# A two-layer hybrid-head decoder on one core: NSA's SBUF pool opened below mLSTM's instead of above it

## The chip, the core and the metric

The kernel runs on one core of one Trainium2 chip. The core has engines that work side by side and each take their instructions in a fixed order: TensorE (PE: matmuls and transposes; PEld is its weight load), VectorE (DVE), ScalarE (ACT), GpSimd (POOL) and SyncE (SP, which here only issues transfers). They meet at semaphores; SBUF is the working memory, PSUM holds matmul results. The metric is the device time of one execution in microseconds (us). All times below come from the runs of the kernel before and from one profiled execution of it.

## The reference, cut to what is computed

Two layers over 512 tokens of width 1024, float32. Each layer projects the normed input to four mixers of four heads of width 64 each, adds their joint output projection to the residual, then adds a cross attention over 256 memory rows and a SwiGLU of width 2816.

```python
for layer in range(2):
    cols = rms_norm(x, g) @ w_in               # split into the four mixers' columns
    m0 = hgrn2_mixer(...)   # gated linear recurrence in chunks of 64, then norm and gate
    m1 = dsa_mixer(...)     # an index picks the top keys of each query, attention over them
    m2 = nsa_mixer(...)     # compressed, selected and windowed attention, gated
    m3 = mlstm_mixer(...)   # matrix-memory recurrence in chunks of 64, then norm and gate
    x = x + concat(m0, m1, m2, m3) @ w_out
    x = x + cross_attention(rms_norm(x), mem)
    x = x + swiglu(rms_norm(x))
```

## The kernel before, in words

**Products.** The residual lives in SBUF transposed, as eight tiles `xT` of 128x512. Each float32 product is made of three matmuls on halves: `xh`,`xl` are the high and low part of an operand, `wh`,`wl` those of a weight (lines L339 to L341 where tokens come out on rows, L329 to L331 where features do; the latter take 128x512). `wh` is written by ACT (L292), `wl` by POOL (L293) from a raw tile `wr` (L277); some weights are split once and come back from memory later (`whl`, L303).

**Stages of a layer.** Stage A interleaves the DSA index and its selection (DVE, L696 and L697), NSA, mLSTM and all input projections. Stage B follows: `load_x` fetches the residual again into `xT` (L405, eight transfers of 256 KB on SP's queue, which takes them in order with all weight transfers), and then three generators are interleaved by cost: `dsa_attn` (DSA's attention: scores L552, exponentials, products L574, transposed back by L605), `hg` (HGRN2: gates L837 to L841 on DVE, products L856 inside chunks, L902 to L930 across them, output norm and gate `h_g` on DVE), and a chain of `out_stage(0)`, `xa_kv`, `out_stage(1)`. `out_stage(s)` is the part of the output projection that belongs to a mixer pair: stage 0 takes NSA's and mLSTM's results (`mo`: NSA's halves are made by ACT and by DVE in L1277, mLSTM's and HGRN2's are first transposed by PE in L1281), stage 1 takes DSA's, stage 2 HGRN2's and runs with the cross attention that follows. In layer 0 `hg` first loads a mask of levels, `lvf` (L826, two transfers), and casts it on DVE (L827); `h_tf`, which the gates read, takes over the mask's staging slots. DSA's keys are made ready by L716 (sum of squares of its latent `d_ckv`, squared by ACT in L713) and L723 (its product with `wukv`), then by a norm and a rotation on DVE.

**Space.** Pools are stacked on the left side of SBUF; a pool that is opened next lies above the one before, and `left.close()` frees both of stage A's. In the space of NSA and mLSTM stage B then puts, from the bottom, `xT`, the pool of `hg` and the pool `dat` of DSA's attention. `reuse_waits="tile"` makes the first writer of a new tile wait for the last users of just those old tiles that lay where it lies. A tile scheduler orders the instructions of each engine ahead of time, from the priorities that the mixes give and from these waits.

Of the kernel before, what the change touches and what calls it, by code (L numbers as in the profile page):

```python
# [206 lines left out]
class Kernel:  # L207
# [1329 lines left out]
    def run(self):  # L1537
        nc = self.nc
        late = ExitStack()
        for l in range(DEPTH):  # L1540
            self.l = l
            banks = ExitStack()
            self.banks(banks, "ba", tp=1, sc=2, o=1, dt=1, mb=1)
            if l == 0:
                self.load_x(self.i["xT"])
            self.layer_consts()
            if l == 0:
                self.open_sq()
            right, index = ExitStack(), ExitStack()
            self.hqf = self.pool(right, "hgqf", side="right")  # L1550
            self.mo = {2: self.t(self.mp, "mo2", [128, 2, S], bufs=1), 3: self.t(self.mp, "mo3", [128, TB, 256], bufs=1)}
            pd = self.pool(index, "dsa", n2=4, n4=0, side="right")
            self.alias[id(pd)] = {"tp": "dt", "sc": "dt"}
            acc = self.dsa_in(pd)
            if l == 0:
                self.setup()
            self.rstd(row=True)
            if l == 0:
                xd = self.i["xT"]
            else:  # L1560
                xd = self.tc.dram_tile([D, S], FT, name=f"xd{l}")
                for c in range(KC):
                    nc.sync.dma_start(xd[c * 128:c * 128 + 128, :], self.xT[c])
            self.xpool.close()
            late.close()
            late, left = ExitStack(), ExitStack()
            pk = self.pool(late, "keep")
            pm = self.pool(left, "ml", n2=3)
            pn = self.pool(left, "nsa", n2=3, n4=1)
            self.alias[id(pn)] = {}  # L1570
            self.hin = None
            for tb in range(TB):
                with self.first():
                    nc.scalar.activation(self.d_idx[:, tb], acc[tb], AF.Copy, scale=self.rcol[:, tb:tb + 1])
            self.weave((self.chain(self.dsa(pd, pk), self.hg_space(index, right)), COST["dsa"]),
                       (self.chain(self.nsa_in(pn),
                                   self.mix((self.nsa(pn), COST["nsa"]),
                                            (self.chain(self.ml_in(pm),
                                                        self.mix((self.ml(pm), COST["ml"]),
                                                                 (self.chain(self.ml_in2(pm), self.dsa_in2(pk), self.hg_in()), COST["in"]))),  # L1580
                                             COST["mlin"]))),
                        COST["two"]))
            left.close()
            banks.close()
            banks = ExitStack()
            self.banks(banks, "bb", tp=1, sc=1, o=1, dt=1, hb=2)
            self.load_x(xd)
            ph = self.pool(left, "hg", n2=2, n4=0)
            pa = self.pool(left, "dat", n2=3, n4=0)
            px = self.pool(right, "xk", n2=2, n4=1, side="right")  # L1590
            self.alias[id(pa)] = {"tp": "dt"}
            self.attn_done = False
            self.weave((self.dsa_attn(pa), COST["attn"]), (self.hg(ph), COST["hg"]),
                       (self.chain(self.out_stage(0), self.xa_kv(px), self.out_stage(1)), COST["out"]))
            left.close()
            banks.close()
            banks = ExitStack()
            self.banks(banks, "bc", tp=2, sc=2, o=2)
            self.open_sq()
            with ExitStack() as e:  # L1600
                p = self.pool(e, "xa")
                rest = self.xa_in(p)
                right.close()
                self.raws = (self.pool(right, "raw", side="right"), RAWS)
                self.all(self.xa(p, self.pool(e, "xo", side="right"), rest))
            with ExitStack() as e:
                self.ffn(self.pool(e, "ffn"))
            self.raws = (self.wp, 3)
            right.close()
            banks.close()  # L1610
        self.xpool.close()
        late.close()
# [18 lines left out]
```

## Time and profile before

| what | value |
|---|---|
| median of 3 runs | 1689.66 us (1684.8 to 1689.67) |
| the profiled execution | 1688.9 us, of which the span is 1687.1 us |
| mean granted clock of TensorE | 0.972 |
| PE busy | 1607.5 us, 95% of the span |
| DVE, POOL, ACT busy | 924.0, 799.1, 712.5 us (55%, 47%, 42%) |
| chain of work that ended last | PE 84%, DVE 8%, issue 3%, DMA, POOL and ACT 2% each |

PE is busy almost throughout, and its matmuls are the chain that ends last for most of the span. What is left to win or to lose by order alone lies in the some 80 us in which PE stands still, and in the stretches where its clock is granted at half.

### The profile page before, as it was taken

What the parts mean: (1) busy time and instruction counts of PE and PEld (TensorE: products, weight loads), DVE (VectorE), ACT (ScalarE), POOL (GpSimd) and SP (SyncE); (2) the same over time, 40 slices, a digit from 0 to 9 for tenths busy, and PEclk for the clock granted to TensorE, in tenths of its full rate; (3) what the DMA queues carried; (4) which work ended last, traced back from release to release, by engine and by line L of the source; (5) the groups of instructions that cost most, each with busy time, mean ns of one, the idle gap of its engine ahead of it and who ended that gap; (6) DMA issues with size and microseconds to landing.
All of it is one profiled execution on the core that took longest, in us unless ns stands there. A gap on an engine that the chain in (4) does not pass through costs nothing.

```text
span 1687.1 us, 25484 instructions
## 1 busy us (share of the span) xinstructions
PE 1607.5 (95%) x9256; PEld 1333.1 (79%) x9262; DVE 924.0 (55%) x1760; ACT 712.5 (42%) x1525; POOL 799.1 (47%) x698
## 2 busy tenths in 40 slices
PE   7899998998899989999999999989998999999999
PEld 7778877777788868888898887677877888888887
DVE  5697688876755330344225884879786644123420
ACT  5555453454654443443324433423665433223321
POOL 5664333456448888874412010144672344444442
PEclk9999997999999999999999999979999999999999
DMA  5342212212338999953355734122131233333331
GB/s 160 89 119 76 70 34 84 57 38 85 112 121 286 305 316 319 333 192 93 105 156 178 262 107 132 58 95 57 45 119 38 66 97 90 92 100 94 94 103 66
DMA packets 114365, 212.72 MB, mean 126 GB/s; under 512 B 12984, under 2 KB 30136, under 8 KB 114240
## 3 DMA queue, kind: packets, MB, share of 16 engines
q1 hardware_dynamic: 111888, 206.11, 38.7%
q10 hardware_dynamic: 2032, 3.94, 0.7%
q8 instruction: 73, 1.20, 0.3%
q0 software_dynamic: 320, 1.05, 0.2%
q14 instruction: 52, 0.43, 0.1%
HBM read 170.69 MB, written 40.35 MB: 125 GB/s over the span
## 4 chain that ended last, share of the span: by engine, by line
PE 84%; DVE 8%; issue 3%; DMA 2%; POOL 2%; ACT 2%; SPq 0%; POOLq 0%; ACTq 0%; DVEq 0%
PE acc L329 14%; PE acc L331 14%; PE acc L330 14%; PE sc L330 5%; PE sc L331 5%; PE sc L329 5%; PE acc L339 3%; PE acc L340 3%; PE acc L341 3%; PE hb L856 3%; PE o L574 2%; PE sc L552 2%; PE tp L493 2%; PE mb L1048 1%; PE dt L493 1%
## 5 line engine op out<-in xcount | busy, mean ns | idle before, releaser
L293 POOL TENSOR_TENSOR wl<-wr,wh 128x512 fp32r<-128x512 f32 (+5 forms) x432 | 551.7, 1285 | 459.3 <-ACT wh L292 447.8
L292 ACT ACTIVATE wh<-wr 128x512 fp32r<-128x512 f32 (+5 forms) x432 | 252.1, 592 | 336.2 <-PE acc L330 149.2
L329 PE MATMUL acc<-xh,wh 128*128 128x512 f32 (+1 forms) x704 | 276.9, 395 | 0.8 <-ACT xh L1283 0.5
L330 PE MATMUL acc<-xl,wh 128*128 128x512 f32 (+1 forms) x704 | 274.6, 390 | 2.9 <-DVE xl L1277 2.9
L331 PE MATMUL acc<-xh,wl 128*128 128x512 f32 (+1 forms) x704 | 275.4, 392 | 0.4 <-POOL wl L293 0.4
L466 DVE TENSOR_TENSOR xT<-acc,xT 128x512 f32<-128x512 f32 (+1 forms) x112 | 68.1, 611 | 214.4 <-PE acc L331 213.6
L329 PEld LDWEIGHTS acc<-xh,wh 128*128 128x128 f32 x704 | 133.9, 191 | 32.1 <-issue 1.7
L330 PEld LDWEIGHTS acc<-xl,wh 128*128 128x128 f32 x704 | 134.3, 191 | 30.8 <-DVE xl L1277 4.0
L331 PEld LDWEIGHTS acc<-xh,wl 128*128 128x128 f32 x704 | 134.1, 190 | 28.7 <-POOL wl L293 1.1
L329 PE MATMUL acc<-f_gh,wh 128*128 128x512 f32 x352 | 139.1, 397 | 6.8 <-ACT f_gh L1491 6.8
L339 PE MATMUL acc<-wh,xh 128*128 128x256 f32 (+2 forms) x480 | 140.6, 296 | 4.9 <-DMA wh<-whl 3.8
L331 PE MATMUL acc<-f_gh,wl 128*128 128x512 f32 x352 | 139.7, 398 | 0.7 <-POOL wl L293 0.7
L330 PE MATMUL sc<-xl,wh 128*128 128x512 f32 x352 | 139.7, 397 | 0.0
L330 PE MATMUL acc<-f_gl,wh 128*128 128x512 f32 x352 | 139.5, 398 | 0.0
L340 PE MATMUL acc<-wl,xh 128*128 128x256 f32 (+2 forms) x480 | 139.0, 291 | 0.0
L331 PE MATMUL sc<-xh,wl 128*128 128x512 f32 x352 | 139.0, 395 | 0.0
L329 PE MATMUL sc<-xh,wh 128*128 128x512 f32 x352 | 138.0, 393 | 0.0
L341 PE MATMUL acc<-wh,xl 128*128 128x256 f32 (+2 forms) x480 | 137.4, 288 | 0.0
L318 POOL TENSOR_TENSOR phl<-pr,phl 128x512 fp32r<-128x512 f32 (+3 forms) x72 | 95.1, 1321 | 35.0 <-ACT phl L317 31.8
L317 ACT ACTIVATE phl<-pr 128x512 fp32r<-128x512 f32 (+3 forms) x72 | 44.2, 613 | 133.9 <-DMA pr<-in_wst 117.2
L339 PEld LDWEIGHTS acc<-wh,xh 128*128 128x128 f32 x480 | 92.9, 194 | 8.8 <-DMA wh<-whl 4.3
L340 PEld LDWEIGHTS acc<-wl,xh 128*128 128x128 f32 x480 | 93.3, 195 | 1.4 <-issue 0.8
(407 smaller groups left out, 3159.8 us busy)
## 6 DMA issues: line engine op xcount, KB each, us to landing
wr<-in_wst SPq DMA_DIRECT2D x332, 256.0 KB, 2.7
whl<-phl SPq DMA_DIRECT2D x52, 512.0 KB, 3.9
pr<-in_wst SPq DMA_DIRECT2D x52, 256.0 KB, 4.1
wh<-whl SPq DMA_DIRECT2D x52, 256.0 KB, 4.1
wl<-whl SPq DMA_DIRECT2D x52, 256.0 KB, 4.4
wr<-in_wst SPq DMA_DIRECT2D x48, 128.0 KB, 2.2
wr<-in_wst SPq DMA_DIRECT2D x32, 192.0 KB, 2.4
whl<-phl SPq DMA_DIRECT2D x8, 524.0 KB, 3.7
```

The lines of the kernel that those rows point to most:

```text
L292: nc.scalar.activation(hi, raw, AF.Copy)
L293: nc.gpsimd.tensor_tensor(lo, raw, hi.bitcast(FT), op=OP.subtract)
L318: nc.gpsimd.tensor_tensor(both[:, 1], raw, both[:, 0].bitcast(FT), op=OP.subtract)
L329: self.nc.tensor.matmul(acc, wh, xh, start=(j == 0), stop=False)
L330: self.nc.tensor.matmul(acc, wh, xl, start=False, stop=False)
L331: self.nc.tensor.matmul(acc, wl, xh, start=False, stop=(j == n - 1))
L339: self.nc.tensor.matmul(acc, xh[:, s], wh, start=(first and j == 0), stop=False)
L340: self.nc.tensor.matmul(acc, xh[:, s], wl, start=False, stop=False)
L341: self.nc.tensor.matmul(acc, xl[:, s], wh, start=False, stop=(last and j == n - 1))
L466: self.nc.vector.tensor_add(self.xT[c][:, cols], acc, self.xT[c][:, cols])
L493: self.nc.tensor.transpose(p[:rows, j * 128:j * 128 + 128], src(j), self.ident)
L856: nc.tensor.matmul(sc[s0:s1, b + t0:b + t1], kk[po:po + 64, b + s0:b + s1], qq[po:po + 64, b + t0:b + t1], start=True, stop=True)
```

## The change

The two lines that open the pools of stage A in each layer are exchanged, so that NSA's pool lies at the bottom and mLSTM's above it.

```diff
             pk = self.pool(late, "keep")
+            pn = self.pool(left, "nsa", n2=3, n4=1)
             pm = self.pool(left, "ml", n2=3)
-            pn = self.pool(left, "nsa", n2=3, n4=1)
             self.alias[id(pn)] = {}
```

In bytes of a partition, before: mLSTM at 108096 to 144970, NSA from 145024 to 195600. After: NSA at 108096 to 158650, mLSTM at 158656 to 195520. Stage B's tiles keep their places: `xT` at 108096 to 124480, the pool of `hg` at 130624 to 164480, that of DSA's attention at 164544 to 195200. Before, `xT` and most of `hg` lay on mLSTM's tiles and DSA's attention on NSA's; now `xT` and `hg` but for its upper end lie on NSA's, and DSA's attention on mLSTM's. No instruction is added to the computation or taken from it. The waits for old tiles differ, and with them the order on each engine. Three places follow.

**SP and DVE at the start of stage B, layer 0.** SP's rows with what they wait for (in brackets, the queue or engine whose semaphore it is): the first reload of the residual, and the two transfers of the mask. Before:

```order
L405 DMA xT_3248<-in_xT 128x512 [waits DMASW2_49,DVE_49]
...
L405 DMA xT_3255<-in_xT 128x512 [waits DMAHW1_49]
L826 DMA lvf<-in_levels 128x384 [waits DMAHW2_49,PE_49]
L826 DMA lvf<-in_levels 128x256 [waits DMAHW3_49]
L277 DMA wr<-in_wst 128x512 [waits DMAHW4_49,Pool_49]
```

After:

```order
L405 DMA xT_3248<-in_xT 128x512 [waits DMASW2_49,PE_49]
...
L405 DMA xT_3255<-in_xT 128x512 [waits DMAHW6_49]
L1307 DMA memT<-in_memT 128x256 [waits DMAHW7_49,DVE_49]
...
L720 DMA wukv<-in_wukv 128x128 [waits DMAHW1_49]
L826 DMA lvf<-in_levels 128x384 [waits DMAHW2_49]
L826 DMA lvf<-in_levels 128x256 [waits DMAHW3_49,DVE_49]
```

The first reload waited for DVE's last use of an mLSTM tile (`mo<-mo,m_tok`); it now waits for PE's last NSA product (L1161). The memory rows and `wukv` moved behind the reload. On DVE, at the same place, before:

```order
L351 TENSOR_TENSOR kv<-rope_3302,rope_3303 128x4x16
L503 CAST ks<-kv 128x4x64
L351 TENSOR_TENSOR ks<-kv,ks 128x4x64
L374 TENSOR_REDUCE q_st<-sq 128x4
L347 TENSOR_SCALAR rs_ms<-q_st 128x4
L827 CAST lv<-lvf 128x384
L827 CAST lv<-lvf 128x256
L837 TENSOR_SCALAR h_f<-h_tf,lbw 128x512
```

After:

```order
L351 TENSOR_TENSOR mo_106<-mo_106,m_tok 128x4x64
L718 TENSOR_SCALAR d_ckv<-d_ckv,cols 128x512
L827 CAST lv<-lvf 128x384
L827 CAST lv<-lvf 128x256
L837 TENSOR_SCALAR h_f<-h_tf,lbw 128x512
...
L874 TENSOR_TENSOR h_ks_3342<-h_k_3336,h_Fk_3338 128x512
L347 TENSOR_SCALAR rs_ms<-dt 128x4
L351 TENSOR_TENSOR kv<-dt,d_st_3273 128x512
```

The mask and the whole gate block of HGRN2 moved ahead of DSA's keys (`kv`). On PE, likewise, L716 and L723 moved from ahead of HGRN2's value and gate projections into them, and the first scores of DSA (L552) ten matmuls further into `out_stage(0)`.

**PE at the end of stage B, layer 0.** The rows from HGRN2's last products on (L928, L930), with its transposes L1281. Before, with seven L574 and four L605, DSA's last, some 85 rows higher:

```order
L928 MATMUL hb<-h_S_4159,h_q 128x128
L930 MATMUL hb<-h_v,h_aT_3384 128x64
L930 MATMUL hb<-h_v,h_aT_3515 128x64
L1281 MATMUL tp<-kc,h_g 128x128 x8
L329 MATMUL acc<-xh,wh 128x512 x2
L330 MATMUL acc<-xl,wh 128x512
```

After:

```order
L574 MATMUL o<-PT,kv 64x128 x7
L605 MATMUL dt<-kc,stat 64x128 x4
L928 MATMUL hb<-h_S_4133,h_q 128x128
...
L930 MATMUL hb<-h_v,h_aT_3515 128x64
L329 MATMUL acc<-xh,wh 128x512 x2
L1281 MATMUL tp<-kc,h_g 128x128 x4
...
L331 MATMUL acc<-xh,wl 128x512
L1281 MATMUL tp<-kc,h_g 128x128 x2
```

Before, the 48 matmuls of `out_stage(1)` were done between HGRN2's products, and its eight transposes stood together. Now DSA ends later, the 48 stand behind HGRN2's last product, and the transposes lie among them. Layer 1 has the same order at this place, with some transposes `tp<-kc,x_ks` beside.

**SP at the start of stage B, layer 1.** Before, four transfers of split weights (L303) stood in the middle of the reload:

```order
L405 DMA xT_11819<-xd_9031 128x512
L303 DMA wl<-whl_8428 128x512
L303 DMA wh<-whl_8428 128x512
L303 DMA wl<-whl_8546 128x512
L303 DMA wh<-whl_8546 128x512
L405 DMA xT_11820<-xd_9031 128x512
```

After:

```order
L405 DMA xT_11823<-xd_9031 128x512
L1307 DMA memT<-in_memT 128x256 x2
L720 DMA wukv<-in_wukv 128x128
L303 DMA wl<-whl_8428 128x512
L303 DMA wh<-whl_8428 128x512
L303 DMA wh<-whl_8546 128x512
L303 DMA wl<-whl_8546 128x512
```

They stand behind the whole reload now, which again waits for PE's L1161 instead of DVE's `mo<-mo,m_tok`.

**Elsewhere.** At the program's start ACT has one square `xsq` and two exponentials of `lbw` (L804) ahead of the first `wh`, which before stood behind it.

## Rows read from the trace of the kernel before

**Rows 1.** The page: busy time by engine; the chain that ended last.
```profile
PE 1607.5 (95%) x9256; PEld 1333.1 (79%) x9262; DVE 924.0 (55%) x1760; ACT 712.5 (42%) x1525; POOL 799.1 (47%) x698
...
PE 84%; DVE 8%; issue 3%; DMA 2%; POOL 2%; ACT 2%; SPq 0%; POOLq 0%; ACTq 0%; DVEq 0%
```
**Rows 2.** PE's waits over the whole span: us in total, times, longest.
```profile
PE acc L330 <- DVE xl L1277: 2.9, 2, 2.6
...
PE dt L723 <- DVE rs_ms L347: 1.0, 1, 1.0
...
PE hb L856 <- DVE h_q L841: 0.8, 1, 0.8
```
**Rows 3.** SP in order of time, layer 0: start, duration, transfers issued.
```profile
276.32 3.65 SPq L405 DMA_DIRECT2D xT<-in_xT  x8
280.07 0.85 SPq L826 DMA_DIRECT2D lvf<-in_levels  x2
```
**Rows 4.** DVE in order of time, layer 0, start of stage B: start, duration.
```profile
275.87 0.42 DVE L351 TENSOR_TENSOR mo<-mo,m_tok 128x256 f32<-128x256 f32 x1
...
285.31 2.35 DVE L827 CAST lv<-lvf 128x384 uint8<-128x384 f32 x2 [1.53 <-DMA lvf<-in_levels]
...
289.06 0.68 DVE L841 SCALAR_TENSOR_TENSOR h_q<-h_tq,h_q 128x512 f32<-128x512 f32 x1
```
**Rows 5.** PE in order of time, layer 0, start of stage B.
```profile
258.77 2.08 PE L1161 MATMUL dt<-n_eT,n_vbd 128*128 128x512 f32 x2 [0.69 <-DVE mo L351]
...
303.13 0.80 PE L330 MATMUL acc<-xl,wh 128*128 128x512 f32 x1 [2.57 <-DVE xl L1277]
...
308.31 0.40 PE L330 MATMUL acc<-xl,wh 128*128 128x512 f32 x1
```
**Rows 6.** PE in order of time, layer 0, end of stage B.
```profile
388.83 0.70 PE L605 MATMUL dt<-kc,stat 128*64 128x128 f32 x7
...
392.90 0.39 PE L331 MATMUL acc<-xh,wl 128*128 128x512 f32 x1
...
394.98 0.39 PE L331 MATMUL acc<-xh,wl 128*128 128x512 f32 x1
...
411.94 0.44 PE L1281 MATMUL tp<-kc,h_g 128*128 128x128 f32 x2 [1.75 <-DVE h_g L351]
414.54 0.69 PE L1281 MATMUL tp<-kc,h_g 128*128 128x128 f32 x2 [2.17 <-DVE h_g L351]
415.71 1.22 PE L329 MATMUL acc<-xh,wh 128*128 128x512 f32 x2 [0.47 <-ACT xh L1283]
416.73 0.63 PE L330 MATMUL acc<-xl,wh 128*128 128x512 f32 x1
...
420.57 0.58 PE L331 MATMUL acc<-xh,wl 128*128 128x512 f32 x1
```
**Rows 7.** ACT in order of time: DSA's last rows at that end.
```profile
390.96 0.51 ACT L616 ACTIVATE xh<-spread 128x128 fp32r<-128x128 f32 x2 [1.00 <-DVE spread L351]
```
**Rows 8.** SP in order of time, layer 1, start of stage B.
```profile
1114.09 2.87 SPq L405 DMA_DIRECT2D xT<-xd  x4
...
1118.47 0.38 SPq L303 DMA_DIRECT2D wh<-whl  x1
```
**Rows 9.** PE in order of time, layer 1, same place.
```profile
1122.87 0.58 PE L339 MATMUL acc<-wh,xh 128*128 128x256 f32 x1 [3.79 <-DMA wh<-whl]
...
1127.51 0.29 PE L339 MATMUL acc<-wh,xh 128*128 128x256 f32 x1
```
**Rows 10.** ACT in order of time, the start.
```profile
9.05 0.62 ACT L427 ACTIVATE xsq<-xT 128x512 f32<-128x512 f32 x1
...
10.18 0.29 ACT L804 ACTIVATE lbw<-lbw 128x4 f32<-128x4 f32 x2
```
**Rows 11.** DVE and POOL in order of time, layer 1, HGRN2's gates.
```profile
1118.64 1.75 DVE L841 SCALAR_TENSOR_TENSOR h_q<-h_tq,h_q 128x512 f32<-128x512 f32 x1
...
1118.13 1.72 POOL L293 TENSOR_TENSOR wl<-wr,wh 128x512 fp32r<-128x512 f32 x1
```

## The prediction

> **What bounds the kernel now.** I read the page first: PE is busy for 1607.5 us and carries 84% of the chain that ended last [rows 1]. The change adds no product, so it can act only on the 80 us in which PE stands still and on the time in which its clock is granted at half. Second, the list of PE's waits, for those that lie at the start or end of stage B: `xl` of L1277 2.9 us, `rs_ms` for L723 1.0, `h_q` for L856 0.8 [rows 2]. Third, the engines in order of time around them.
>
> Layer 0. SP issues the reload at 276.32, when DVE's last use of mLSTM's tile ends (275.87 + 0.42), and the mask 3.7 us later at 280.07 [rows 3, 4]. The mask reaches DVE at 285.31: 1.53 us of wait there, and HGRN2's gates come behind it [rows 4]. DVE is then late with `xl`, and PE waits 2.57 us at 303.13, after which its matmuls run slow until 308.31 [rows 5]. At the end of the stage PE waits 1.75 and 2.17 us for `h_g` and 0.47 for its high part, and again runs slow [rows 6].
>
> Layer 1. The reload starts at 1114.09, and the last of four weight transfers that stand in it is issued at 1118.47 [rows 8]. PE waits 3.79 us for one of them, until 1122.87, and is slow until 1127.51 [rows 9].
>
> What slow costs, from rows: in the tail's nine steps from 416.73 to 420.57 one 128x512 matmul starts 0.427 us after the other, in the nine from 392.90 to 394.98 0.231 [rows 6]. These are the clock's two levels, 1.2 and 2.4 GHz, the lower one behind PE's waits. So each slow matmul loses 0.196 us, or a slow stretch 46% of itself.
>
> **The change part by part.**
>
> *Start of stage B, layer 0.* The reload waits for L1161, which ends at 260.85 (258.77 + 2.08) [rows 5], so the mask can be issued some 14 us earlier. From issue to landing it takes 5.2 us now (285.31 less 280.07); it will lie ready before DVE ends `mo` at 276.29. DVE then needs L718 (0.5, estimated from like shapes) and the casts (2.35), so the gates start at about 279 instead of 287.7 (285.31 + 2.35), and the first L856 of HGRN2 finds `h_q`. Removed on PE: the wait for `h_q`, 0.84; the wait at L723, which moves behind projections, 0.98; L723 then runs at full clock, which pays for L716, today hidden in a wait. The `xl` of L1277: DVE comes to it after the gate block, DSA's keys and two steps of POOL, by my count of durations along the new order at 295 to 298. PE, which today stands there from 300.56 (303.13 - 2.57), comes some 4 us earlier, at 296 to 297, since two waits and L723 no longer stand ahead of it. I take the 2.9 as gone and with it the slow stretch 303.13 to 308.31, 5.2 x 46% = 2.4. Sum -7.1. New: POOL does two steps of HGRN2 before the first `wl` of the gate weights; between 0 and 2.7 us of wait, I take 0.7, because PE has other rows in front of it. **-6.4** (bounds -7.1, and -1.1 if `xl` stays late: only 0.84 + 0.98 go, less 0.7).
>
> *End of stage B, layer 0.* 48 matmuls of `out_stage(1)`, 48 x 0.231 = 11.1 us, now lie behind HGRN2's last product. The transposes wait today from 410.19 (411.94 - 1.75), and their inputs come at 411.94 and 414.54, 1.8 and 4.4 us later; in the new order 10 and 16 matmuls (2.3 and 3.7 us) lie between, and their own start adds 1 to 2. So 1.75 + 2.17 + 0.47 = 4.4 go, and the slow stretch 415.71 to 420.57 + 0.58, 5.4 x 46% = 2.5. New: `out_stage(1)` needs DSA's last result. From the last L605 (ends 389.53) to the end of ACT's `xh` (391.47) it takes 1.9 us [rows 6, 7], of which two L928 and four L930 cover 0.9: +1.0. DSA's last softmax has fewer other rows in between: 0 to 2, I take +0.6. **-5.3** (bounds -6.9 and -2).
>
> *Start of stage B, layer 1.* The weight transfers stand behind all eight reloads, but these start 17 us earlier, when L1161 ends at about 1096.4. The weights then wait only for the matmuls that free their buffers (about 1113, from the projections' place in the order); issued then and landing in 4 to 5 us they are there at 1117.5 to 1118.5, about when PE wants them (1119.1, 3.79 before 1122.87). Gone: 3.8 and the slow stretch 1122.87 to 1127.51, 4.64 x 46% = 2.1. Residue 0 to 4, I take 0.6. **-5.3** (bounds -5.9 and -1).
>
> *End of stage B, layer 1.* Here PE does not wait for `h_g` today, so nothing is won, and DSA's last result is waited for with less cover: **+1.2** (0 to 2.5).
>
> *The start of the program.* One `xsq` and two `lbw` steps, 0.62 + 0.29 [rows 10], come ahead of the first `wh`, which releases PE's first matmul: **+0.9** (0 to 1.2; zero if another operand is later).
>
> *The middle of both stages.* DSA's keys and its queries stand further back on DVE, ACT and POOL; its attention and HGRN2's blocks are mixed anew. The trace of before has no row for this. Below it is nothing; above, four query blocks a layer, each at worst 2 us late (as the waits of rows 5 and 6 are): 16. I take **+3**, nearer to zero, since in the new order L521 and L552 still stand behind some ten matmuls of other work each.
>
> Sum: -6.4 - 5.3 - 5.3 + 1.2 + 0.9 + 3 = -11.9 on the profiled execution's 1688.9, so 1677.0. The median of the runs shown is 0.8 above that execution: **1678 us**, 0.7% faster. A measurement of this kernel can tell a change of about 0.3%, 5 us.
>
> What row speaks against the first part: DVE's L841 takes 0.68 us at 289.06 [rows 4] but 1.75 at 1118.64, beside POOL's `wl` (1118.13, 1.72) [rows 11]. In the new order the gate block runs beside POOL's steps. If four of its ten instructions are stretched by 1.0 us each, `xl` comes at 299 to 302 and PE waits for it as today. The Trainium skill has a rule for it (GPSIMD Engine Reference, Specifications): GpSimd's way into SBUF is shared with VectorE, and they contend where a DVE instruction has two SBUF inputs. L841 has two, and the rows agree. By the rule taken strictly, the `xl` wait and its slow stretch stay, and the sum is 1683.
>
> **The rivals.**
> 1. *The wait at `xl` stays* (or, the same in size, the weights of layer 1 land late). For it: the stretched L841 [rows 11]. Against: the gates' 8 us of advance. It takes back 2.9 + 2.4 = 5.3: 1683.
> 2. *Nothing to measure.* The places gain, but the middle costs 9 to 15 us instead of 3, so the sum is near zero: 1689. For it: DSA begins its queries later in a stage that PE fills. Against: PE's order is fixed, and nothing is on it that must wait so long.
> 3. *Slower: DSA's chain becomes the bound.* The place is `out_stage(1)`, which cannot begin before the last L605. Today 26.2 us lie between that (389.53) and the first HGRN2 matmul of the output (415.71). In the new order 1.0 + 1.0 + 11.1 + 1.6 for transposes, 14.7, must lie there, so DSA may end up to 11.5 us later than today, 14 with the slow stretch saved, before the layer loses. Beyond this each us of DSA is one of the kernel's. By the order its keys come some 10 us later (the square of the latent stands behind mLSTM's end). If it loses 8 more on the way, its last L605 comes 18 us later; 18 less 14 leaves 4 to 5 in each layer, and what the starts gain only moves PE's wait: about 1698. Against: DSA's rows are spread over the whole stage, and its last ones alone are moved.
> 4. *The change does nothing of the kind*, because the reload's new wait isn't the earlier one. The order shows the semaphore of PE there; I give it no chance of its own.
>
> **How the numbers follow.** Forecast (1671 to 1683) 0.56; rival 1 0.17; rival 2 0.14; rival 3 0.13. Faster by over 0.3% (below 1684.6): the forecast and two thirds of rival 1, 0.67; within: 0.06 + 0.14 = 0.20; slower 0.13. The range must leave out no more than 2 in 10: 1670 below (all of the middle's 3 gone and each place at its better bound, with some to spare), 1691 above, which takes in rivals 1 and 2.
>
> **What the changed profile would show.** Right: the reload issued near 261 and 1096; no DVE wait for `lvf`; gates at 279, L856 at 281 to 282; no wait of PE over 1 us for `xl` L1277, `h_g` L351 or `wh<-whl`; full clock at 415 to 421 and after 1119. A stage B 10 us shorter in layer 0 and 4 in layer 1. Wrong: PE waits at L552 or L493 in the middle of stage B, at L329 behind DSA's `xh`, or at L340 for POOL's `wl`; or the same waits as before under other lines. What would upset the forecast most is a clock that falls at a place that is fast today.

## The result, and the profile after

The changed kernel takes **1666.51 us** (median of 6 runs, 1663.43 to 1668.55); before takes 1689.43 beside it (6 runs). The ratio is 0.987, with an interval of 0.985 to 0.989. The forecast was 1678, range 1670 to 1691: the direction was right, the gain twice what was forecast. (Beside the kernels below, `before` has medians of 1685.7 to 1687.0, so the gain is nearer 20 us than 23.) The profiled execution after takes 1668.55 us, its span is 1666.8, so the two profiles differ by 20.3 us.

The page after, for [rows 1]: PE is busy 8.8 us less with the same products.

```profile
PE 1598.7 (96%) x9262; PEld 1326.0 (80%) x9262; DVE 920.8 (55%) x1760; ACT 711.5 (43%) x1525; POOL 799.8 (48%) x698
...
PE 82%; DVE 9%; issue 2%; DMA 2%; POOL 2%; ACT 2%; SPq 0%; ACTq 0%; POOLq 0%; DVEq 0%
```

PE's waits over the whole span, for [rows 2]: `xl` of L1277, `rs_ms` for L723, `h_q` and `h_g` are gone from the list, and so is the wait for layer 1's split weights [rows 9]; the 0.6 that is still listed for them lies at 952.23, in stage A. The wait for `mo` at the start of layer 0's stage B has grown from 2.5 to 4.1, and the 0.3 for DSA's `xh` (L616) lies in layer 1. First the line of `mo` before, then the lines after:

```profile
PE tp L1281 <- DVE mo L351: 2.5, 1, 2.5
```

```profile
PE tp L1281 <- DVE mo L351: 4.1, 1, 4.1
...
PE acc L339 <- DMA wh<-whl: 0.6, 1, 0.6
...
PE acc L329 <- ACT xh L616: 0.3, 1, 0.3
```

Where the 20 us lie is read from windows with equal work at both ends: from stage A's last product (L1065) to the first sum of `out_stage(2)` (L466), on to the first sum of the cross attention's output, and the same in layer 1. Columns: window, its length, busy time (and count) of PE, PEld, DVE, ACT, POOL, then the granted clock, the DMA share and GB/s. Before:

```profile
268.43:421.07 152.64, 140.63 (x1007) 117.33 (x1010) 112.20 (x230) 68.63 (x170) 83.39 (x95) 0.93 0.24 72
421.07:467.41 46.34, 40.55 (x295) 34.31 (x296) 34.73 (x70) 31.14 (x78) 21.26 (x20) 0.93 0.34 106
1107.73:1250.09 142.36, 137.63 (x1006) 116.19 (x1009) 110.96 (x222) 65.18 (x165) 80.45 (x90) 0.97 0.25 75
1250.09:1299.81 49.72, 42.51 (x297) 35.98 (x297) 38.06 (x69) 31.48 (x79) 25.49 (x23) 0.90 0.29 86
```

After:

```profile
268.33:411.33 143.00, 136.82 (x1008) 114.60 (x1009) 112.04 (x231) 68.92 (x172) 85.95 (x95) 0.97 0.22 64
411.33:459.00 47.67, 41.34 (x297) 34.16 (x297) 34.62 (x69) 30.94 (x76) 22.46 (x20) 0.96 0.35 103
1096.23:1231.31 135.08, 134.11 (x1009) 113.29 (x1009) 106.02 (x223) 66.38 (x167) 82.46 (x93) 0.98 0.23 67
1231.31:1279.84 48.53, 42.25 (x297) 34.84 (x297) 34.73 (x70) 31.59 (x77) 21.37 (x20) 0.93 0.25 77
```

Stage B of layer 0 is 9.6 us shorter and the piece behind it 1.3 longer; layer 1's pieces are 7.3 and 1.2 shorter. That is 16.8. Of the rest 1.9 lie in the feed-forward part of layer 0, 1.2 in stage A of layer 1, 0.4 elsewhere. In both stages the gain has two halves: PE stands still less (12.0 to 6.2, 4.7 to 1.0), and it is busy for less time (3.8 and 3.5) at a higher mean clock (0.93 to 0.97, 0.97 to 0.98).

SP at both starts, for [rows 3, 8]: the reloads are issued at 260.67 and 1086.26, the mask and the split weights behind them have nothing to wait for in the queue.

```profile
260.67 4.79 SPq L405 DMA_DIRECT2D xT<-in_xT  x8
...
266.97 1.05 SPq L826 DMA_DIRECT2D lvf<-in_levels  x2
...
1086.26 3.64 SPq L405 DMA_DIRECT2D xT<-xd  x8
...
1101.90 0.33 SPq L303 DMA_DIRECT2D wl<-whl  x1
1102.32 0.86 SPq L303 DMA_DIRECT2D wh<-whl  x2
```

DVE at the start of layer 0's stage B, for [rows 4]: the casts start without a wait and the gates at 277.64 (287.7 before).

```profile
276.50 0.72 DVE L827 CAST lv<-lvf 128x384 uint8<-128x384 f32 x2
277.64 0.55 DVE L837 TENSOR_SCALAR h_f<-h_tf,lbw 128x512 f32<-128x512 f32 x1 [0.41 <-ACT h_tf L836]
...
294.78 0.69 DVE L1277 TENSOR_TENSOR xl<-mo,xh 128x512 fp32r<-128x512 f32 x1
295.39 1.40 DVE L503 CAST ks<-kv 128x256 fp32r<-128x256 f32 x1
296.71 1.75 DVE L1277 TENSOR_TENSOR xl<-mo,xh 128x512 fp32r<-128x512 f32 x1
```

PE at the end of that stage, for [rows 6]: DSA's last product, HGRN2's last, and transposes of `h_g` among the matmuls of `out_stage(1)`, with no wait. The 128x512 matmuls from 397.58 on start 0.23 us apart, at the full clock.

```profile
394.37 0.70 PE L605 MATMUL dt<-kc,stat 128*64 128x128 f32 x7
...
395.99 0.56 PE L930 MATMUL hb<-h_v,h_aT 128*128 128x64 f32 x4
396.36 0.71 PE L329 MATMUL acc<-xh,wh 128*128 128x512 f32 x2
396.91 0.60 PE L1281 MATMUL tp<-kc,h_g 128*128 128x128 f32 x4
...
397.58 0.39 PE L331 MATMUL acc<-xh,wl 128*128 128x512 f32 x1
397.81 0.39 PE L329 MATMUL acc<-xh,wh 128*128 128x512 f32 x1
```

### The profile page after: what moved, and what is told of

It reads as the page before. It is cut to its first block, busy times and chain, and to the rows that moved or that the text cites. A ratio compares the mean times of both kernels' runs of the same rounds, so it can differ in the third digit from the quotient of the medians.

```text
span 1666.8 us, 25488 instructions
## 1 busy us (share of the span) xinstructions
PE 1598.7 (96%) x9262; PEld 1326.0 (80%) x9262; DVE 920.8 (55%) x1760; ACT 711.5 (43%) x1525; POOL 799.8 (48%) x698
## 4 chain that ended last, share of the span: by engine, by line
PE 82%; DVE 9%; issue 2%; DMA 2%; POOL 2%; ACT 2%; SPq 0%; ACTq 0%; POOLq 0%; DVEq 0%
PE acc L329 13%; PE acc L331 13%; PE acc L330 13%; PE sc L330 5%; PE sc L331 5%; PE sc L329 5%; PE acc L339 4%; PE acc L340 3%; PE acc L341 3%; PE hb L856 2%; PE o L574 2%; PE sc L552 2%; PE tp L493 2%; POOL wl L293 1%; PE mb L1048 1%
## 5 line engine op out<-in xcount | busy, mean ns | idle before, releaser
L466 DVE TENSOR_TENSOR xT<-acc,xT 128x512 f32<-128x512 f32 (+1 forms) x112 | 67.8, 610 | 215.7 <-PE acc L331 215.5
```

The costliest lines, as they stand in the source:

```text
L466: self.nc.vector.tensor_add(self.xT[c][:, cols], acc, self.xT[c][:, cols])
```

## The experiments

The table gives each kernel's time, its ratio to the executions of before that were taken beside it, with the interval, and from its profile the two **pieces**: from stage A's last L1065 to the first sum of the cross attention's output (the two windows above together), with the time in which PE stands still. A piece comes from one execution. Where a layer is left as it was, it repeats within 2.2 us (layer 0: 199.0, 201.2, 200.3; layer 1: 192.1, 191.8). Whole executions spread more: 24 of before take 1681.6 to 1697.6.

| kernel | median, us (runs) | ratio | layer 0: piece (idle) | layer 1: piece (idle) |
|---|---|---|---|---|
| before | 1689.43 (6) | 1 | 199.0 (17.8) | 192.1 (11.9) |
| after | 1666.51 (6) | 0.987 [0.985, 0.989] | 190.7 (12.5) | 183.6 (7.2) |
| layer0_only | 1673.85 (5) | 0.9918 [0.9889, 0.9948] | 191.4 (13.3) | 191.8 (12.0) |
| layer1_only | 1680.28 (10) | 0.9953 [0.9929, 0.9977] | 201.2 (18.8) | 183.0 (8.2) |
| reload_on_act | 1675.1 (8) | 0.9928 [0.9901, 0.9955] | 191.6 (15.2) | 195.8 (13.9) |
| attn_cost_42 | 1690.52 (10) | 1.0021 [1.0001, 1.0042] | 200.8 (17.4) | 193.1 (10.9) |
| mask_ahead | 1687.76 (10) | 1.0000 [0.9984, 1.0017] | 206.4 (18.2) | 187.3 (10.9) |
| l1_weights_ahead | 1680.0 (8) | 0.9962 [0.9938, 0.9986] | 200.3 (19.1) | 184.8 (9.2) |
| after_reload_late | 1674.69 (4) | 0.9933 [0.9907, 0.9958] | 195.1 (15.1) | 189.5 (11.2) |
| after_out_cost_26 | 1668.54 (4) | 0.9892 [0.9872, 0.9911] | 189.6 (13.4) | 188.4 (11.5) |
| mask_and_weights | 1684.53 (10) | 0.9993 [0.9979, 1.0007] | 201.2 (17.7) | 183.2 (7.6) |
| after_mask_stage_a | 1673.86 (4) | 0.9931 [0.9907, 0.9954] | 192.3 (13.7) | 189.3 (11.2) |
| start_and_tail | 1689.4 (10) | 1.0022 [1.0008, 1.0035] | 199.4 (16.6) | 192.3 (11.4) |
| start_tail_weights | 1683.63 (10) | 0.9976 [0.9956, 0.9996] | 199.5 (16.6) | 183.3 (9.1) |
| reload_on_pool | 1680.99 (10) | 0.9957 [0.9938, 0.9975] | 191.5 (10.7) | 195.3 (13.4) |
| late_reload_both | 1681.51 (10) | 0.9972 [0.9950, 0.9994] | 202.0 (19.2) | 182.5 (8.6) |
| mask_in_stage_a | 1697.18 (5) | 1.0061 [1.0040, 1.0082] | 201.9 (17.2) | 196.5 (13.3) |

**The change in one layer.** Both pools' lines under `if l == 0` (layer0_only) or `if l == 1` (layer1_only), the old order in the other layer.

> The two pools are exchanged in layer 0 alone. Theory (the time comes from the two starts of stage B, where the reload and what stands behind it no longer wait for mLSTM, and from layer 0's covered tail): layer 0 alone gives some 10 us, as the trace with both layers has stage B of layer 0 9.6 us shorter, and layer 1 keeps its 3.8 us wait for wh<-whl; about 1679.5. Rival A (one layer carries it, the other's gain is only shifted): near 1689 or near 1667. Rival B (the gain is spread over all stages by a new order everywhere): neither layer alone reaches half.

> The two pools are exchanged in layer 1 alone. Theory: 7.3 us in stage B of layer 1 and about 1 to 2 behind it; about 1680, with layer 0's waits for xl, h_q and h_g as before. Rival A: near 1689 or near 1667. Rival B: less than a third of the 23 us.

Each layer's piece goes to its value of after and the other stays: 10.6 us of the profile in one, 11.2 in the other, of which 2.1 lie ahead of layer 1's stage B. The layers add. Layer 1's piece alone is worth 9 us, where the forecast had 2.6. layer0_only's median lies 6 us below what was expected of it, layer1_only's where it was expected.

**The queue in layer 1.** The pools stay as before; the reload's tiles are first written by a small copy of HGRN2's values, so that the reload itself must wait for them.

```diff
+        if self.nx > 2:
+            for c in range(KC):
+                self.nc.vector.tensor_copy(self.xT[c][:, 0:1], self.h_v[:, TB - 1, 0:1])
```

> Pools as before; in layer 1 one element of each reload tile is first copied from the last of HGRN2's value tile, so that the reload waits for that and the four weight transfers stand ahead of it; DVE has eight small copies more. Layer 0 is as before. Theory: the wait for wh<-whl of 3.8 us and the slow stretch behind it go, 5 us in layer 1 less 1 for the copies; 1682 to 1683 beside 1687. The other 3 to 4 us that the exchanged pools gave layer 1 don't come, as the waits for mLSTM's space stay. Rival (all of layer 1's gain is this queue's order): 1678 to 1679. Second rival (the late reload is waited for by the residual's sum): 1688 or more.

SP in that kernel (lines 3 higher) issues the weights first:

```profile
1111.24 0.33 SPq L303 DMA_DIRECT2D wl<-whl  x1
1111.66 1.24 SPq L303 DMA_DIRECT2D wh<-whl  x2
...
1119.95 0.79 SPq L408 DMA_DIRECT2D xT<-xd  x2
```

PE no longer waits for `wh<-whl`, and the piece shrinks by 7.3, nearly what the whole change gives this layer, without its pools; 6.0 of it lie in stage B (142.4 to 136.3), the rest in the cross attention behind. The median, 1680.0, lies between the theory's figure and the rival's. Three more kernels have the weights ahead of the reload in layer 1 with the old pools (mask_and_weights, start_tail_weights, late_reload_both): 182.5 to 183.3. All others with the old pools in that layer lie at 187.3 to 196.5; of these only reload_on_act (below) has the weights first as well, and pays elsewhere. The others all have a wait of 2.6 to 3.8 for `wh<-whl`, so their spread of 9 us has causes beside that wait: mask_ahead keeps 3.6 of it at 187.3.

**The queue in layer 0, three ways.** reload_on_act and reload_on_pool issue the reload elsewhere; mask_ahead lowers the reload's rank so that the mask is issued first. In all three the pools lie as before, where by its addresses less than half of the pool of `hg` (130624 to 144970, of 130624 to 164480) lies on mLSTM's tiles, not most of it as was said above.

```diff
-            eng = self.nc.sync if self.nx > 1 else ...
+            eng = self.nc.scalar if self.nx > 1 else ...
```

> Pools as before; the eight reloads of each layer are issued by ACT instead of SP, so that nothing on SP stands behind them. They wait for mLSTM's tiles as before. Theory (what stood behind the reload on SP is what cost): layer 1's wait for wh<-whl of 3.8 us and its slow stretch go, and the mask of layer 0 comes early; 5 us from layer 1, 2 to 4 from layer 0's start, and the tail of layer 0 as its order comes out; 1677 to 1684. Rival (the space for HGRN2's tiles itself, not the queue, held the stage): no more than 2 us, 1687 or more; ACT's issues (0.45 us each) could also cost 2 to 4 us there.

```diff
+            with self.tc.high_priority(offset=-300) if self.nx > 1 else ExitStack():
+                eng.dma_start(self.xT[c], src[c * 128:c * 128 + 128, :])
```

> Pools as before; the reload has a lower priority, so that in layer 0 the mask's two transfers stand ahead of the eight reloads on SP. The space is as before: HGRN2's tiles still wait for mLSTM's. In layer 1 five reloads stand ahead of the four weight transfers, so that place stays. Theory (the mask behind the reload is what held layer 0's start): layer 0 gives most of what its start gave with the exchanged pools, 5 to 7 us, by its first HGRN2 product 5 us earlier and no wait for lvf; the wait for h_g stays; 1680 to 1682 beside a before of 1687. Rival (space and order, not the mask): within 2 us of before.

With the reload on ACT layer 0 gains 7.4 with the old pools, and layer 1 gives 3.7 back (a new wait of 1.9 for `h_v`, which ACT makes, and 1.3 for `xl`; the one for the split weights is down to 0.6). That execution, 1683.19, is 8 us above the median of its eight, so what layer 1 loses may belong to it alone. mask_ahead measured nothing, against its expectation: the mask is issued at 266.10 and the gates start at 276.77, but the tail's wait for `h_g` is still there (3.7), and PE's clock falls behind another wait, on a stretch most of which was fast before (from 308.31 on [rows 5]). PE and the windows there (lines 1 higher):

```profile
303.58 0.93 PE L857 MATMUL hb<-h_qs,h_k 64*128 64x128 f32 x6 [0.94 <-DVE h_aT L351]
```

```profile
296.00:306.00 10.00, 9.02 (x51) 6.81 (x49) 9.80 (x14) 4.41 (x9) 6.46 (x5) 0.98 0.34 105
306.00:316.00 10.00, 9.96 (x37) 8.11 (x38) 6.79 (x18) 3.01 (x11) 1.74 (x2) 0.50 0.01 2
```

PE was busy for 9.96 of these 10 us, at 1.2 GHz.

**The tail in layer 0.** `"attn": 42.00` in COST instead of 49.42, the pools as before.

> Pools as before; the cost number of DSA's attention is 42 instead of 49.42, which makes DSA end later in the order, so that in layer 0 out_stage(1) lies behind HGRN2's last products and its transposes lie among it, as with the exchanged pools. Theory: the tail of layer 0 is a gain by itself, 4 to 5 us (waits for h_g of 3.9 and a slow stretch of 2.5 go, 1 to 2 come back for DSA's late end), while xl 2.9 and wh<-whl 3.8 stay: 1684 to 1686. Rival (the tail's waits go only because the stage starts earlier): no change, 1689; or DSA's chain becomes late and it is slower.

The `h_g` wait left the list, the kernel did not get faster: the start kept `xl` (2.8), and a wait of 2.1 for `wl` came at 429.85, in the cross attention behind the stage. Stage B itself is only 1.4 shorter: PE stands still 2.9 us less there, and is busy 1.5 us longer although its mean clock is higher (0.95 against 0.93). So neither edit by itself earns. Both together, by these two edits, and with layer 1's weights:

> The pools as before, with the edits of mask_ahead and attn_cost_42 together: the mask of levels is issued ahead of the reload in layer 0, and DSA's attention is interleaved at the lower cost, so that 23 matmuls of out_stage(1) stand between DSA's last product and HGRN2's last, and 12 more ahead of the first h_g transpose, where before all 48 stood ahead of HGRN2's last product. Theory: a late start and a waiting tail of stage B are each enough to lose the stage (each opened alone measured nothing: ratios 1.0000 and 1.0021), and both open give layer 0 what the change gives it: its stage B takes 142 to 146 us instead of 152.6, the kernel 1676 to 1680 (layer 1 as before or 3 better). Rival: nothing adds to nothing, the gain of layer 0 hangs on something else in the new order: 1686 to 1691, stage B over 150 us.

> The pools as before, with the edits of mask_and_weights and attn_cost_42 together: in layer 0 the mask ahead of the reload, in layer 1 the split weights ahead of the reload, in both the tail opened by the lower cost of DSA's attention. Theory: the three waits are what the change removes; layer 0's stage B 142 to 146 us and layer 1's start without the wait of 3.6 us: 1668 to 1673, most of the change's gain without its pools. Rival: the places do not add, since mask_and_weights measured 1684.5 where the sum asked for 1680: 1680 to 1686.

Here my theory failed as I had put it: layer 0 stays at 199.4. It is no clean test. `xl` is down to 0.6, but `ks` 1.2 and `h_aT` 0.9 are new at the start, 2.4 for `wl` in the cross attention, and the tail isn't quiet. PE's waits there, from 396 to 419, and the window (lines 1 higher):

```profile
PE tp L1282 <- DVE h_g L351: 1.0, 1, 1.0
PE acc L329 <- ACT xh L1284: 0.6, 1, 0.6
```

```profile
410.00:418.00 8.00, 6.36 (x20) 4.15 (x18) 4.84 (x7) 2.71 (x7) 3.88 (x5) 0.79 0.51 157
```

But waits are the smaller part of it. The window of its whole stage B, to be held against those of before and after above:

```profile
267.46:418.36 150.90, 142.00 (x1008) 117.00 (x1010) 117.55 (x231) 67.14 (x168) 83.61 (x93) 0.96 0.23 71
```

It is 7.9 us longer than after's. PE stands still 2.7 us more (8.9 against 6.2), and is busy 5.2 us more (142.0 against 136.8). By an estimate from the stretches at half clock, some 2 of that are the clock's. What else makes the same products dearer is shown only in part. In after HGRN2's L856 start 96 ns apart where sixteen stand together and 126 where eight do, at the full clock:

```profile
296.47 1.71 PE L856 MATMUL hb<-h_q,h_k 64*128 64x128 f32 x16
...
300.89 1.16 PE L856 MATMUL hb<-h_qs,h_k 64*128 64x128 f32 x8
```

So a new order can cost PE time without any wait. By an estimate from the starts in the traces, the 192 products of this form in layer 0 take 24.7 us in start_and_tail and 25.4 in attn_cost_42, 23.2 in before, 23.5 in after and 21.8 in reload_on_act; the rest of the 5.2 is open.

In layer 1 the weights gave 9.0 again (192.3 to 183.3).

**Start open with the tail shut or open.** Three more kernels with the old pools, told apart ahead of the run by PE's order at the tail: reload_on_pool (the reload on `gpsimd`) has matmuls of `out_stage(1)` behind HGRN2's last product, late_reload_both (l1_weights_ahead's edit with `self.nx > 1`) and mask_in_stage_a (the mask's load and casts moved into stage A) have none.

> The pools as before; the reload of the residual is issued on GpSimd's queue instead of SP's, in both layers. In the order that this gives, seven matmuls of out_stage(1) stand between DSA's last product and HGRN2's last, and four more ahead of the first h_g transpose (48 and 0 before), and the mask is no longer behind the reload. Theory: layer 0 gains where the start and the tail are both opened and the tail loses its slow stretch, as with the reload on ACT: from the end of stage A to the first product after the cross attention's start 190 to 194 us instead of 199.0; layer 1's weights are no longer behind the reload, 183 to 187 there instead of 192.1; 1671 to 1678. Rival: layer 0's gain hangs on the order that the pools give and not on these two places; then 198 to 202 in layer 0 and 1679 to 1684 in all.

> The pools as before; the edit of l1_weights_ahead in both layers, so that the reload also stands behind the mask and the first raw weights in layer 0. In layer 0's tail 47 matmuls still stand ahead of HGRN2's last product and none behind it. Theory: with the start open and the tail shut layer 0 gains nothing, 198 to 203 us in the same piece; layer 1 183 to 186; 1679 to 1684. Rival: the queue at the start is what layer 0 gains by, whatever the tail; then 190 to 195 in layer 0 and 1671 to 1676 in all.

> The pools as before; the mask of levels is loaded and cast in stage A, so that nothing of it lies behind the reload in layer 0. The tail has 47 matmuls ahead of HGRN2's last product and none behind it, and layer 1 is as before. Theory: start open, tail shut, no gain in layer 0: 198 to 203 us in that piece, 1685 to 1691. Rival as for late_reload_both: 190 to 195 there, 1677 to 1682.

The layer-0 pieces came as the theory had them: 191.5, 202.0, 201.9. PE's waits at the tail of reload_on_pool (396 to 416), then of late_reload_both (396 to 425, lines 3 higher):

```profile
PE sc L339 <- ACT xh L438: 0.9, 1, 0.9
```

```profile
PE tp L1284 <- DVE h_g L351: 3.9, 2, 2.2
PE acc L329 <- ACT xh L1286: 0.5, 1, 0.5
```

With the tail shut the early start is lost again on the way: late_reload_both's first L856 comes 7.3 us earlier, its piece is 3 longer, with 2.6 of wait for `ks` in the place of `xl`. On totals the theory was wrong twice. mask_in_stage_a takes 1697.2, above its 1685 to 1691: layer 1, where nothing was edited, lost 4.4. In reload_on_pool layer 1 keeps a wait of 2.6 for `wh<-whl` and loses 3. The weights are no longer behind the reload there, but they are issued at 1108.97 to 1110.46, while the eight transfers of the reload go out on the other queue (1105.70 to 1110.34), and they take 8.2 us to land; in l1_weights_ahead, where the reload starts 7 us behind the last of them, 3.9. Columns: number, size, median us from issue to landing, between 1098 and 1131, of reload_on_pool, then of l1_weights_ahead:

```profile
wh<-whl SPq DMA_DIRECT2D x2, 256.0 KB, 8.2
```

```profile
wh<-whl SPq DMA_DIRECT2D x2, 256.0 KB, 3.9
```

It looks as if not only the order in one queue counts, but also what is under way beside the weights; no run varies that alone.

**Both at once**, the mask ahead in layer 0 alone and the weights ahead in layer 1:

> The pools as before; in layer 0 the mask of levels is issued ahead of the reload (the edit of mask_ahead, for that layer alone), and in layer 1 the split weights ahead of the reload (the edit of l1_weights_ahead). Theory: the two queues are separate, and what a queue gives in layer 0 is lost again when the clock falls behind a wait of some 0.9 us at 303 with small products after it, as in mask_ahead; the order there is much the same, so it falls again: 1680 (1678 to 1682), a granted clock of about 0.5 in 306 to 316. Rival: the fall in that profile was of one execution and not of the order; then layer 0 keeps 4 to 6 us of its earlier gates: 1674 to 1677, and a full clock in 306 to 316. Second rival: the queues are not what the gain is made of; then no more than 3 us: 1684 to 1687.

Layer 1 gave 8.9 in the profile, layer 0 lost 2.2. That execution, 1679.76, is among the shortest of its ten, and the median lies above the first range, in that of the second rival; the granted clock in 306 to 316 is 0.86, between the two figures that were named.

**The changed kernel taken further or undone.** after_reload_late: one reload tile is first written from `mo`, so that one of the eight transfers, and what stands behind it on SP, waits for mLSTM again; the other seven go early.

```diff
+        if self.nx > 1:
+            self.nc.vector.tensor_copy(self.xT[0][:, 0:1], self.mo[3][:, TB - 1, 255:256])
```

> Pools exchanged; one of the eight reload tiles is first touched by DVE from mLSTM's last result, so that it and, behind it on SP, the mask (layer 0) or the four weight transfers (layer 1) wait for mLSTM again. Theory (what is queued behind the reload costs): most of the gain of the two starts is lost, 5 us in layer 0 and 4 to 5 in layer 1; 1675 to 1678 beside 1666 for the exchanged pools alone. Rival (the space itself): within 2 us of the exchanged pools, 1666 to 1668.

DVE waits 2.61 us for `lvf` again and PE 1.2 for `xl`; 4.4 of layer 0's 8.3 and 5.9 of layer 1's 8.5 are lost. That execution, 1679.62, is the longest of its four. How much hangs on the reload's wait can't be read from it. In layer 0 the mask is issued late (273.90), but HGRN2's first L856 comes 15.6 us behind stage A's last L1065, as in after (15.3; 21.4 before); stage B is 2.0 longer than in after, and the other 2.4 lie in the cross attention, at a lower clock. In layer 1 PE has no wait for the split weights. It has one for `mo` (lines 2 higher):

```profile
PE tp L1283 <- DVE mo L351: 3.8, 1, 3.8
```

The next two kernels leave the reload alone and have the same wait of 3.8 in layer 1, where after has none; their layer 1 takes 188.4 and 189.3, as here 189.5. So what this layer lost goes with that wait, and not with the reload's.

after_out_cost_26 (`"out": 26.0`) and after_mask_stage_a (the mask moved as in mask_in_stage_a, on the changed kernel):

> Pools exchanged; the cost number of the output stages is 26 instead of 21.47, so that they move up in the mix. Theory: the gaps left at the stage's end and start are small (under 1 us in layer 1, DSA's end in layer 0), so it can give at most 2 us; 1664 to 1668, no change that can be measured. Rival: DSA's late end is still worth several us, 1660 to 1662.

> The changed kernel, and besides the mask of levels is loaded and cast already in stage A, in staging slots of the weights, so that neither its transfers nor its two casts lie at the start of stage B of layer 0. Theory: with the reload early no one waits for the mask any more (no DVE wait for it in the changed profile), and the casts' 0.7 us lie behind other work: within 2 us of the changed kernel, 1665 to 1669. Rival: DVE is still the late engine at that start, since the gates stand behind the casts; then 2 to 4 us are earned, 1662 to 1665.

Neither beats the change. The second is 7 us slower, outside what either theory allowed: layer 1's start now has the wait of 3.8 for `mo`, though the edit is in layer 0. A new order in one place moved the other.

## Why the prediction was wrong in size

*Start of stage B, layer 0 (-6.4): right.* Reload, mask, gates (277.64, forecast 279) and the first L856 (283.66, forecast 281 to 282; it starts 6.1 us earlier than before) came nearly as said, and the waits for `h_q`, `rs_ms` and `xl` with the slow stretch behind the last went, 7.1 in all. The 0.7 for POOL's `wl` didn't come; 1.6 more for `mo`, which the forecast had not, did. **Rival 1** was close: `xl` is made at 294.78 and 296.71, the second stretched to 1.75 beside POOL's `wl` as the rule of the Trainium skill (GPSIMD Engine Reference, Specifications) has it, and the trace agrees. PE was not there yet, which is in part luck: it comes to these products at 298.45, 2.1 us earlier than before, not the 4 of the forecast, and the second `xl` ends at 298.46. At 296 to 297, as forecast, PE would have had to wait for it.

*End of stage B, layer 0 (-5.3): right, and better than said.* 4.4 of waits and the slow stretch are gone, 6.9 in all; DSA's last L605 ends 5.5 us later than before, far from rival 3's 14, and PE shows no wait for what follows from it in this layer, so the 1.6 set against the gain didn't come. The two places and half of the middle made -10.2; the window shows -9.6, and 1.3 of it is given back in the cross attention. The sum came near by errors that offset each other: 7.1 less 1.6 and 6.9 make 12.4, so some 3 us were lost in the middle, where the forecast had 1.5. An estimate from the traces agrees: counted by PE's products done, each at its mean step in this stage, after is 6 us ahead of before at a quarter of the stage, 2 to 3 at nine tenths, 10 at its end.

It seems that the two hang together, which I had not seen; this isn't shown. Seven kernels (after, after_*, layer0_only, reload_on_act and reload_on_pool) wait at most 1.3 us at a time at the start, but for `mo`, and at most 0.4 for `h_g`: 189.6 to 195.1. Of the other ten eight have the tail's waits or the start's. start_and_tail and start_tail_weights don't fit: they wait at most 1.3 at the start and 1.0 for `h_g`, hardly more than the seven, and PE's busy time is what they lose by. All ten lie at 199.0 to 206.4. What the runs show is less: with the old order at the tail an early start alone gained nothing in four kernels (mask_ahead, mask_and_weights, late_reload_both, mask_in_stage_a), eaten up by new waits, by a clock that falls elsewhere, or by products that PE takes longer over.

*Start of stage B, layer 1 (-5.3): the mechanism right, the size a little small.* 3.8 of wait and 2.1 of slow stretch make 5.9. Moving the weights ahead, and nothing else in this layer, shortens the stage by 6.0 to 6.8 against before (l1_weights_ahead, mask_and_weights, late_reload_both), and the whole piece by 7.3 to 9.6, since the cross attention behind the stage shrinks too, which the forecast had not counted (in after PE's clock there goes from 0.90 to 0.93).

*The step that failed* is layer 1's sum, where costs were set against that gain: +1.2 for its end, +1.5 for its middle (half of the +3), 0.6 of residue. None of them came. PE's waits in layer 1's stage B are 1.0 us in all, and its busy time there fell by 3.5, where the slow stretch had 2.1. The forecast's 2.6 for this layer (5.3 less 1.2 less 1.5) stands against 7.3 in the stage and 8.5 with the piece behind. The middle, which I put at +3 without a row of its own, cost some 3 us in layer 0 and nothing in layer 1. The +0.9 for the program's start came and was lost again: the first product starts 1.2 later (9.20 to 10.41), but by 51 us into the span the difference is 0.1. In the profiles the sum misses by 8.4: layer 1 gained 5.9 more than forecast, layer 0 1.9 less, and all the rest 4.4 more (3.5 gained where 0.9 was to be lost).

The range had no room for that. With every cost at nothing and each place at its better bound (7.1, 6.9 and 5.9) the sum is 1669.8, so 1670 had nothing to spare, as no bound allowed a gain outside the three places.

*Outside the sum* lie 1.2 in stage A of layer 1 and 1.9 in the feed-forward part of layer 0. Both are within what other kernels show where nothing was edited: from layer 0's feed-forward to layer 1's last L1065 late_reload_both, with the old pools, is 2.2 us shorter than before, and from layer 0's piece to the end of its feed-forward the other profiles stand 3.7 below to 1.0 above that of before. I count them to order and to single executions. The medians differ by 2.6 more than the profiles, since the profiled execution of after is the longest of its six.

*Left open.* No kernel has the start shut and a wholly quiet tail, so what the tail is worth by itself isn't known. Nor is it settled how much of the change's order in layer 0 comes from the removed wait and how much is luck of the scheduler. That the queue can be enough is shown: with the old pools and the reload off SP's queue layer 0 gains 7.4 and 7.5. So is that it need not be: mask_ahead and late_reload_both opened it too, and gained nothing there.

The largest loss left at this place in after is the wait for `mo`, 4.14 us; no kernel here removes it.

```profile
272.47 0.87 PE L1281 MATMUL tp<-kc,mo 128*128 128x128 f32 x3 [4.14 <-DVE mo L351]
```

## What to carry to other kernels

Where a queue takes transfers in order, look at what the first one waits for: the place of a tile in memory decides it, and a late small transfer behind it can cost more than its own wait. Two stalls in one stage may not add up when the engine between them is full: test them together, and look at that engine's busy time beside its waits, since a new order can make the same products dearer. Put no cost on what no row shows without the same chance of a gain. After any edit that lets a scheduler reorder, compare piece by piece, since an edit in layer 0 moved layer 1 by 5.7 us.

## What the runs showed of the hardware

A wait of 0.94 us was followed by 10 us and more at half clock (mask_ahead, 0.50 granted from 306 to 316), while after_reload_late, with a wait of 1.19 us at about the same place (for `xl`, 297.59 to 298.78), stayed at the full clock from 296 to 306 and on. The Trainium skill (TensorE: Matmul & The Clock Gate, HAM oscillation) has that gaps in PE's work bring the clock down; these runs agree that they may, and the length of the gap alone doesn't tell which one will.

DVE's casts are stretched beside POOL as much as its sums of two operands: L503 takes 1.40 us at 295.39 beside `wl`, and 0.29 at 1127.52, where POOL stands still. The Trainium skill (GPSIMD Engine Reference, Specifications) counts a DVE instruction in a two-port performance mode among those that contend with GpSimd, which would cover it; the trace agrees, though it doesn't show the mode.
